# Two steps of an attention branch at a time, keys and values in turn

## The chip, the cores and the metric

One Trainium2 chip, one of its cores. The metric is the device time of one execution in microseconds. Engine names as in the profile: PE (TensorE matmul), PEld (its weight loads), DVE (VectorE), ACT (ScalarE), POOL (GpSimd), SP (the queue that issues most DMAs).

## What is computed

One layer of a decoder trunk over 512 positions, width 1024. A projection feeds two attention branches, A (8 query heads, one key and value head, an indexer that chooses the 128 best keys of each query, a bias by distance) and B (8 heads with up-projected latents, dense causal attention), which are gated, summed, projected and followed by an MLP. Shortened:

```python
h = rmsnorm(x, attn_norm_g)
a_q, a_k, a_v, i_q, i_k, i_w, c_q, c_kv, k_r, g = split_cols(h @ w_in, IN_SIZES)
# A: top_k of the indexer's scores, then attention over the chosen keys
score = einsum('bqh,bqhs->bqs', iw, relu(einsum('bqhd,bsd->bqhs', iq, ik) * 64 ** -0.5))
_, sel = top_k(where(causal, score, -inf), 128)
logits = einsum('bqhd,bqkd->bqhk', q, k[sel]) * 64 ** -0.5 + rel_table[rel_bucket(pos_q - pos[sel])]
y_a = einsum('bqhk,bqkd->bqhd', softmax(where(valid, logits, -1e30)), v[sel])
# B: queries and keys of 64 + 32 (rotary) per head
logits = (einsum('bqhd,bshd->bhqs', q_nope, k_nope) + einsum('bqhr,bsr->bhqs', q_rope, k_rope)) * 96 ** -0.5
y_b = einsum('bhqs,bshd->bqhd', softmax(where(causal, logits, -1e30)), v_b)
gates = sigmoid(g + b_gate)
x = x + (gates[:, :, 0] * (y_a @ w_branch_a) + gates[:, :, 1] * (y_b @ w_branch_b)) @ w_out
x = x + square(relu(rmsnorm(x, mlp_norm_g) @ w_ff1)) @ w_ff2
out = rmsnorm(x, final_norm_g)
```

## The kernel before

The order of PE's instructions is the order in which the program writes them; the other engines' instructions are put in order by the framework, by its own estimate of when each is ready, and each engine then works its list through in that order. Precision is kept by splitting: a matrix is a high part and a rest, and a product is three matmuls (high by high, high by rest, rest by high; `mm3`, L143 to L145, and L239 to L241). A weight is loaded raw by SP (`pre`, L114), ACT writes the high part (L121), DVE the rest (L123); for the weights in `pool_lo` POOL writes the rest. `use` starts this two weights ahead of the matmuls.

The kernel runs in stages. The first projection (L175 to L194) works on slices of `xT` and `wsr` as they land, after `NWARM` small matmuls on zeros. Then come the indexer's scores, the queries of B, and the key and value stage (L553 to L573, about 76 to 91 us): four key chunks (matmuls into `pl`, DVE scales them to `kf`, POOL copies half to `kh`, ACT and DVE write the parts `kth` and `ktl`), then four value chunks that ACT reads into `vb`. PSUM has two buffers `pa`, three `pl`, two `pt` and one `po`.

The B stage (L636 to L652, 91 to 161 us) has 32 steps of one head and one block of 128 queries, and `BL` = 7 more. A step is `b_s0` (three wide matmuls into `pl` and a mask matmul of 16-bit floats, then the softmax: DVE's maximum `nmx`, ACT's exponential `pr`, DVE's reciprocal `rs`, POOL's scaling L592), in each second step of a head `b_q` (four transposes for the next head's queries into `pt`), `b_s1` of the step seven back (transposes of the softmax into `pt`, ACT copies them to `ptb`), and a piece of a gate's projection (`fb`, usually three wide matmuls L239 to L241 into `pa`). After each second head `b_pv` multiplies by the values into `po`, which ACT and DVE read as `ybh` and `ybl`. `topk` gives DVE rounds of the selection (L402, L403), which the framework may put anywhere after their inputs.

The four chunks of A's queries (L670 to L683, 161 to 197 us, the `qa` stage) go into `pa`; DVE scales them to `qf`, ACT and DVE write the parts `qa`; two gate chunks follow. The A stage (L744 to L756, 197 to 275 us) has 32 units of 16 queries, 8 for each block, the longest first. `a_oh` has DVE write four comparisons (`oh`) for a unit; `a_s0` runs two wide matmuls (L705, L706), a mask matmul (L707) and twelve matmuls (L711) of 32 output rows, of which four work side by side, the last two kinds on 16-bit floats, then the softmax; `a_s1` transposes three units later (`LAG`); `fa` is a piece of a gate. After a block `a_av` multiplies by the values. What follows (275 us to the end) is the merging of branches, the output projection and the MLP.

## Time and profile before

| | us |
|---|---|
| median of 3 runs | 723.49 (723.43 to 723.56) |
| profiled execution | 723.43 |
| its span, first to last instruction | 721.7 |
| start to B stage | 91.3 |
| B stage | 69.7 |
| `qa` stage and two gate chunks | 36.0 |
| A stage | 78.4 |
| after it | 446.3 |

A start in a timeline is us from the span's start. A duration of PE includes the time in which a matmul runs beneath the next one, so the cost of one is the distance to the next start. A square bracket holds the idle time of the engine before the instruction and what ended it.

### The profile page before, as it was taken

Reading aid. Unit: us, or ns where it says so; the run is one execution under the profiler, and the core shown is the slowest. Engines: PE = TensorE matmul, PEld = TensorE weight load, DVE = VectorE, ACT = ScalarE, POOL = GpSimd, SP = SyncE. Lnnn points to the kernel's source line nnn. Section 1 sums busy time; section 2 is a strip of 40 time slices with the busy share of each in tenths; the row PEclk is TensorE's granted clock in tenths of the full one; section 3 lists DMA queues with packets and bytes.
Section 4 is the critical chain, followed back from the end, with each engine's and each line's share of the span. In section 5 each row is a group of like instructions: output and inputs, shape, how many; then the busy total and the mean of one; then the engine's idle time right before and its main releaser. Section 6 shows DMA issues by size and latency. Waiting matters only on the chain.

```text
span 721.7 us, 9980 instructions
## 1 busy us (share of the span) xinstructions
PE 707.3 (98%) x3725; PEld 569.7 (79%) x3726; DVE 430.2 (60%) x810; ACT 305.7 (42%) x533; POOL 192.0 (27%) x230
## 2 busy tenths in 40 slices
PE   8999999999899999999999999999999999999996
PEld 7879777778656677888898888888888888888885
DVE  6487899999898865773257353353534425335233
ACT  6466676655544555761156041240514215025013
POOL 2315287530065430332224011020201202012012
PEclk9999999999999999999999999999999999999998
DMA  8532522112221118882046152150412405111002
GB/s 335 202 110 89 153 89 74 45 48 94 84 67 45 46 47 277 322 271 62 1 151 202 56 153 80 66 168 17 167 51 88 145 30 176 29 59 59 0 18 99
DMA packets 25952, 77.16 MB, mean 107 GB/s; under 512 B 3568, under 2 KB 4464, under 8 KB 25904
## 3 DMA queue, kind: packets, MB, share of 16 engines
q1 hardware_dynamic: 24896, 75.19, 31.1%
q10 hardware_dynamic: 1008, 1.34, 0.5%
q8 instruction: 29, 0.48, 0.3%
q14 instruction: 19, 0.16, 0.1%
HBM read 69.31 MB, written 6.29 MB: 105 GB/s over the span
## 4 chain that ended last, share of the span: by engine, by line
PE 87%; DVE 8%; ACT 2%; issue 1%; POOL 1%; DMA 1%; POOLq 0%; SPq 0%; ACTq 0%; DVEq 0%
PE pa L143 10%; PE pa L145 9%; PE pa L144 9%; PE pl L143 9%; PE pl L145 9%; PE pl L144 9%; PE pa L239 4%; PE pa L240 4%; PE pa L241 4%; PE pl L711 2%; DVE sc L403 2%; PE pt L724 2%; PE pa L822 2%; PE pa L821 2%; PE pa L820 2%; DVE m L402 2%
## 5 line engine op out<-in xcount | busy, mean ns | idle before, releaser
L121 ACT ACTIVATE whi<-wraw 128x1024 fp32r<-128x1024 f32 (+1 forms) x103 | 107.9, 1053 | 216.1 <-PE pl L145 88.6
L123 DVE TENSOR_TENSOR wlo<-wraw,whi 128x1024 fp32r<-128x1024 f32 (+1 forms) x98 | 124.9, 1283 | 80.3 <-ACT whi L121 79.8
L875 POOL TENSOR_TENSOR sq<-r 128x512 f32<-128x512 f32 x32 | 49.3, 1543 | 244.3 <-ACT r L873 244.3
L143 PE MATMUL pa<-h2h,whi 128*128 128x512 f32 (+1 forms) x272 | 102.5, 377 | 0.0
L144 PE MATMUL pa<-h2l,whi 128*128 128x512 f32 (+1 forms) x272 | 102.4, 377 | 0.0
L145 PE MATMUL pa<-h2h,wlo 128*128 128x512 f32 (+1 forms) x272 | 102.4, 377 | 0.0
L144 PE MATMUL pl<-wlo,zh 128*128 128x512 f32 (+1 forms) x260 | 100.3, 386 | 0.0
L145 PE MATMUL pl<-whi,zl 128*128 128x512 f32 (+1 forms) x260 | 100.3, 386 | 0.0
L143 PE MATMUL pl<-whi,zh 128*128 128x512 f32 (+1 forms) x260 | 100.3, 386 | 0.0
L890 DVE SCALAR_TENSOR_TENSOR acc<-pl,r,acc 128x512 f32<-128x512 f32 (+1 forms) x65 | 48.2, 741 | 85.8 <-PE pl L145 85.8
L239 PE MATMUL pa<-hh,whi 128*128 128x512 f32 x184 | 79.3, 431 | 2.2 <-DVE qf L673 2.2
L240 PE MATMUL pa<-hl,whi 128*128 128x512 f32 x184 | 72.1, 392 | 0.0
L241 PE MATMUL pa<-hh,wlo 128*128 128x512 f32 x184 | 72.1, 392 | 0.0
L145 PEld LDWEIGHTS pa<-h2h,wlo 128*128 128x128 f32 x272 | 51.2, 188 | 9.4
L143 PEld LDWEIGHTS pa<-h2h,whi 128*128 128x128 f32 x272 | 51.2, 188 | 9.3
L144 PEld LDWEIGHTS pa<-h2l,whi 128*128 128x128 f32 x272 | 51.2, 188 | 9.3
L145 PEld LDWEIGHTS pl<-whi,zl 128*128 128x128 f32 x260 | 48.8, 188 | 9.9
L144 PEld LDWEIGHTS pl<-wlo,zh 128*128 128x128 f32 x260 | 48.8, 188 | 9.8
L143 PEld LDWEIGHTS pl<-whi,zh 128*128 128x128 f32 x260 | 48.8, 188 | 9.8
L592 POOL TENSOR_SCALAR pra<-pra,rs 128x400 f32<-128x400 f32 (+31 forms) x32 | 33.0, 1032 | 61.1 <-DVE rs L591 60.7
L696 DVE TENSOR_SCALAR oh<-posbc,thr 128x400 bf16<-128x400 f32 (+31 forms) x128 | 43.0, 377 | 3.5 <-PE pl L711 3.5
L239 PEld LDWEIGHTS pa<-hh,whi 128*128 128x128 f32 x184 | 35.2, 191 | 11.0 <-issue 6.4
(294 smaller groups left out, 1204.3 us busy)
## 6 DMA issues: line engine op xcount, KB each, us to landing
wraw<-wff SPq DMA_DIRECT2D x64, 512.0 KB, 3.6
wraw<-wF SPq DMA_DIRECT2D x24, 512.0 KB, 3.4
gd<-gt SPq DMA_DIRECT2D x16, 256.0 KB, 2.2
wraw<-wbr SPq DMA_DIRECT2D x8, 512.0 KB, 4.0
wraw<-wout SPq DMA_DIRECT2D x8, 512.0 KB, 5.1
gx<-gd SPq DMA_DIRECT2D x16, 256.0 KB, 3.7
xtok<-x SPq DMA_DIRECT2D x4, 512.0 KB, 9.9
acc<-x SPq DMA_DIRECT2D x1, 2048.0 KB, 9.6
```

The lines of the kernel that those rows point to most:

```text
L121: act.activation(hi, raw, AF.Copy)
L123: eng.tensor_tensor(lo, raw, hi.bitcast(F32), op=ALU.subtract)
L143: pe.matmul(ps, lh, rh, start=(i == 0), stop=False)
L144: pe.matmul(ps, lh, rl, start=False, stop=False)
L145: pe.matmul(ps, ll, rh, start=False, stop=(i == n - 1))
L239: pe.matmul(p, h[:, k], hh[k], start=(k == 0), stop=False)
L240: pe.matmul(p, h[:, k], hl[k], start=False, stop=False)
L241: pe.matmul(p, l[:, k], hh[k], start=False, stop=(k == NK - 1))
L592: pool.tensor_scalar(pr, pr, rs, None, op0=ALU.mult)
L696: dve.tensor_scalar(oh[:, :n], posbc[:, :n], thr[:, 4 * G + q:4 * G + q + 1], None, op0=ALU.is_le)
L875: pool.tensor_tensor(sq, r, r, op=ALU.mult)
L890: dve.scalar_tensor_tensor(acc[:, b, cs], p, r2[:, b:b + 1], acc[:, b, cs], op0=ALU.mult, op1=ALU.add)
```

## The change

Nine edits. (1) The first piece of `xT` is loaded by SP, after the first `wsr`, not by ACT ahead of `vec`; `NWARM` is 52, not 46. (2) `pool_lo` also holds the two gate chunks behind the `qa` stage and the four chunks of A's queries. (3) In the key and value stage a value chunk follows each key chunk; the copy into `kh` is ACT's and the one into the odd heads' `kth` POOL's, in place of the other way round. (4) `b_q` transposes into `po`, not `pt`. (5) The B loop takes two steps at a time: both tiles' wide matmuls, then both masks, then both softmaxes; two `b_s1`; `b_q` with a head's first pair; two fills. `BL` is 6. (6) `topk` gives 26 rounds in the B loop, not 27. (7) The A loop takes two units at a time in the same way (wide, mask, the `L711` kind), with the comparisons of the next pair after it; `LAG` is 2, so `a_s1` runs for the pair before. (8) `oh` has 12 buffers, not 8. (9) `qh` is in the pool of four buffers that `qf` and the gates use.

```diff
--- before.py
+++ after.py
@@ -43,7 +43,8 @@
     return ap.to_broadcast(shape)


-NWARM = 46
+NWARM = 52
+OHB = 12


 def body(nc, tc, ctx, a, out, dbg=lambda name, ap: None):
@@ -129,7 +130,7 @@
     seq += gl[NG1 + 1:NG1 + NG2 + NGB] + [("in", 4 + i) for i in range(4)] + gl[NG1 + NG2 + NGB:]
     seq += [("br", i) for i in range(NK)] + [("ff1", i) for i in range(32)]

-    pool_lo = set(gl[NG1 + NG2:NG1 + NG2 + NGB])
+    pool_lo = set(gl[NG1 + NG2:NG1 + NG2 + NGB + NGQ] + [("in", 4 + i) for i in range(4)])

     def use(key, ahead=2):
         i = seq.index(key)
@@ -151,7 +152,6 @@
     hl = Two(2, F32R, "hl")
     vec = cst.tile([128, 52], F32, name="vec")
     xT = [utile(4 + i, F32, f"xT{i}") for i in range(2)]
-    act.dma_start(xT[0][:, 0:1], a["xT"][:, 0:1])
     act.dma_start(vec, a["vec"])
     warm = cst.tile([128, 1], F32, name="warm")
     dve.memset(warm, 0.0)
@@ -175,8 +175,7 @@
     for nk in (1, 1, 2, 2, 2):
         ks = slice(k, k + nk)
         sp.dma_start(wsr[:, ks], a["wS"][:, ks])
-        if k:
-            sp.dma_start(xT[k // 4][:, k % 4:k % 4 + nk], a["xT"][:, ks])
+        sp.dma_start(xT[k // 4][:, k % 4:k % 4 + nk], a["xT"][:, ks])
         for kk in range(k, k + nk):
             xk = xT[kk // 4][:, kk % 4]
             if kk:
@@ -535,7 +534,7 @@
         sp.dma_start(kth[64:96, h].bitcast(F32), kth[64:96, 0].bitcast(F32))
         sp.dma_start(ktl[h][64:96].bitcast(F32), ktl[0][64:96].bitcast(F32))
     def b_q(h):
-        pt = pt_tile()
+        pt = psO.tile([128, NB, 128], F32, tag="po", name="pq")
         for b in range(NB):
             pe.transpose(pt[:96, b], qtok[:, b, h], ident)
         ptq = pt[:96].rearrange("p a b -> p (a b)")
@@ -557,20 +556,18 @@
         t = t_p.tile([128, S], F32, tag="s2k", name="kf", bufs=4)
         dve.tensor_tensor(t, p, rkbc, op=ALU.mult)
         th = t_p.tile([128, S], F32R, tag="s2k", name="kh", bufs=4)
-        pool.tensor_copy(th[64:128], t[64:128])
+        act.activation(th[64:128], t[64:128], AF.Copy)
         act.activation(kth[0:64, 2 * j], t[0:64], AF.Copy)
-        dve.tensor_tensor(ktl[2 * j][0:64], t[0:64], kth[0:64, 2 * j].bitcast(F32), op=ALU.subtract)
-        act.activation(kth[0:64, 2 * j + 1], th[64:128].bitcast(F32), AF.Copy)
-        kt_last = dve.tensor_tensor(ktl[2 * j + 1][0:64], t[64:128], th[64:128].bitcast(F32), op=ALU.subtract)
-        f2(2)
+        dve.tensor_tensor(ktl[2 * j + 1][0:64], t[64:128], th[64:128].bitcast(F32), op=ALU.subtract)
+        kt_last = dve.tensor_tensor(ktl[2 * j][0:64], t[0:64], kth[0:64, 2 * j].bitcast(F32), op=ALU.subtract)
+        pool.tensor_copy(kth[0:64, 2 * j + 1], th[64:128].bitcast(F32))
+        f2(1.5)
         if j == 2:
             b_q(0)
-    for b in range(NB):
-        sl = slice(b * 128, (b + 1) * 128)
         p = pl_tile()
-        mm3(p, [(zkh[:, sl], zkl[:, sl], ukh[:, 512:1024], ukl[:, 512:1024])])
-        act.activation(vb[:, b], p, AF.Copy, scale=rlat[:, 4 + b:5 + b])
-        f2(1.5)
+        mm3(p, [(zkh[:, cs], zkl[:, cs], ukh[:, 512:1024], ukl[:, 512:1024])])
+        act.activation(vb[:, j], p, AF.Copy, scale=rlat[:, 4 + j:5 + j])
+        f2(2)
     dbg("vb", vb)
     z_st.close()

@@ -596,17 +593,23 @@
     prs, ptbs = {}, {}
     yb = []

-    def b_s0(h, b):
-        n = 128 * (b + 1)
-        pl = pl_tile()
-        qh, ql = (t[:, b * 128:n] for t in qts[h])
-        pe.matmul(pl[:, :n], qh, kth[:, h, :n], start=True, stop=False)
-        pe.matmul(pl[:, :n], qh, ktl[h][:, :n], start=False, stop=False)
-        pe.matmul(pl[:, :n], ql, kth[:, h, :n], start=False, stop=False)
-        pe.matmul(pl[:, b * 128:n], identb, nm0, start=False, stop=True)
-        pr = b2_p.tile([128, n], F32, tag=f"pr{b}", name=f"pr{b}", bufs=3)
-        softmax_rows(pl, n, pr)
-        prs[h, b] = pr
+    def b_s0(h, bb):
+        pls = {}
+        for b in bb:
+            n = 128 * (b + 1)
+            pl = pls[b] = pl_tile()
+            qh, ql = (t[:, b * 128:n] for t in qts[h])
+            pe.matmul(pl[:, :n], qh, kth[:, h, :n], start=True, stop=False)
+            pe.matmul(pl[:, :n], qh, ktl[h][:, :n], start=False, stop=False)
+            pe.matmul(pl[:, :n], ql, kth[:, h, :n], start=False, stop=False)
+        for b in bb:
+            n = 128 * (b + 1)
+            pe.matmul(pls[b][:, b * 128:n], identb, nm0, start=False, stop=True)
+        for b in bb:
+            n = 128 * (b + 1)
+            pr = b2_p.tile([128, n], F32, tag=f"pr{b}", name=f"pr{b}", bufs=3)
+            softmax_rows(pls[b], n, pr)
+            prs[h, b] = pr

     def b_s1(h, j):
         if j == 0:
@@ -631,24 +634,26 @@
         dve.tensor_tensor(ybl[:, h0 // 2], po, ybh[:, h0 // 2].bitcast(F32), op=ALU.subtract)

     f2.flush()
-    BL = 7
+    BL = 6
     fb = Fill(gtake(NGB), 32 + BL)
-    for t in range(32 + BL):
+    for t in range(0, 32 + BL, 2):
         h, i = divmod(t, 4)
         if h < 8:
-            b_s0(h, 3 - i)
-        if i == 1 and h + 1 < 8:
-            b_q(h + 1)
+            b_s0(h, (3 - i, 2 - i))
         h1, j = divmod(t - BL, 4)
         if t >= BL:
             b_s1(h1, j)
-        fb()
+            b_s1(h1, j + 1)
+        if i == 0 and h + 1 < 8:
+            b_q(h + 1)
         if t == 4:
             with tc.issue_after(kt_last.ins):
                 topk(1)
-        elif t > 4 and t % 4:
             topk(1)
-        if j == 1 and h1 >= 2 and h1 % 2 == 0:
+        elif t > 4:
+            topk(1 if i == 0 else 2)
+        fb(2)
+        if j == 0 and h1 >= 2 and h1 % 2 == 0:
             b_pv(h1 - 2)
     fb.flush()
     b_pv(6)
@@ -672,7 +677,7 @@
             t = t_p.tile([128, S], F32, tag="s2k", name="qf", bufs=4)
             dve.scalar_tensor_tensor(t, p, 0.125, r1bc, op0=ALU.mult, op1=ALU.mult)
             tq = t.rearrange("p (g q) -> p g q", q=4)
-            th = a_p.tile([128, S], F32R, tag="qh", name="qh", bufs=1)
+            th = t_p.tile([128, S], F32R, tag="s2k", name="qh", bufs=4)
             act.activation(th[64:128], t[64:128], AF.Copy)
             act.activation(qa[0:64, :, 0, :, j], tq[0:64], AF.Copy)
             act.activation(qa[0:64, :, 1, :, j], tq[64:128], AF.Copy)
@@ -692,29 +697,37 @@
         G = 8 * b + g
         ohs = oht[b, g] = []
         for q in range(4):
-            oh = a_p.tile([128, S], BF16, tag="oh", name="oh", bufs=8)
+            oh = a_p.tile([128, S], BF16, tag="oh", name="oh", bufs=OHB)
             dve.tensor_scalar(oh[:, :n], posbc[:, :n], thr[:, 4 * G + q:4 * G + q + 1], None, op0=ALU.is_le)
             ohs.append(oh)

-    def a_s0(b, g):
-        n = 128 * b + 16 * (g + 1)
-        G = 8 * b + g
-        ohs = oht[b, g]
-        pl = pl_tile()
-        lq = qa[:, 4 * G:4 * G + 4].rearrange("p a b c d -> p (a b c d)")
-        pe.matmul(pl[:, :n], lq, ak[:, 0, :n], start=True, stop=False)
-        pe.matmul(pl[:, :n], lq, ak[:, 1, :n], start=False, stop=False)
-        pe.matmul(pl[:, :n], esel[:, 4 * g:4 * g + 4].rearrange("p a b c d -> p (a b c d)"), nms[b][:, :n],
-                  start=False, stop=False)
-        for i in range(3):
-            for q in range(4):
-                pe.matmul(pl[32 * q:32 * q + 32, :n], dtab[:, i].rearrange("p a b c -> p (a b c)"), ohs[q][:, :n],
-                          start=False, stop=(i == 2))
-        pr = a_p.tile([128, S], F32, tag="pra", name="pra", bufs=5)
-        if g < 7:
-            pool.memset(pr[:, n:128 * (b + 1)], 0.0)
-        softmax_rows(pl, n, pr[:, :n])
-        pas[b, g] = pr
+    def a_s0(us):
+        pls = []
+        for b, g in us:
+            n = 128 * b + 16 * (g + 1)
+            G = 8 * b + g
+            pl = pl_tile()
+            pls.append(pl)
+            lq = qa[:, 4 * G:4 * G + 4].rearrange("p a b c d -> p (a b c d)")
+            pe.matmul(pl[:, :n], lq, ak[:, 0, :n], start=True, stop=False)
+            pe.matmul(pl[:, :n], lq, ak[:, 1, :n], start=False, stop=False)
+        for (b, g), pl in zip(us, pls):
+            n = 128 * b + 16 * (g + 1)
+            pe.matmul(pl[:, :n], esel[:, 4 * g:4 * g + 4].rearrange("p a b c d -> p (a b c d)"), nms[b][:, :n],
+                      start=False, stop=False)
+        for (b, g), pl in zip(us, pls):
+            n = 128 * b + 16 * (g + 1)
+            for i in range(3):
+                for q in range(4):
+                    pe.matmul(pl[32 * q:32 * q + 32, :n], dtab[:, i].rearrange("p a b c -> p (a b c)"),
+                              oht[b, g][q][:, :n], start=False, stop=(i == 2))
+        for (b, g), pl in zip(us, pls):
+            n = 128 * b + 16 * (g + 1)
+            pr = a_p.tile([128, S], F32, tag="pra", name="pra", bufs=5)
+            if g < 7:
+                pool.memset(pr[:, n:128 * (b + 1)], 0.0)
+            softmax_rows(pl, n, pr[:, :n])
+            pas[b, g] = pr

     def a_s1(b, g):
         if g == 0:
@@ -739,20 +752,21 @@
     Fill(gtake(NGQ), 1).flush()
     fa = Fill(gtake(NGA), 34)
     ua = [(b, g) for b in (3, 2, 1, 0) for g in range(8)]
-    LAG = 3
+    LAG = 2
     a_oh(*ua[0])
-    for i in range(len(ua) + LAG):
-        topk(1)
-        if i + 1 < len(ua):
-            a_oh(*ua[i + 1])
+    a_oh(*ua[1])
+    for i in range(0, len(ua) + LAG, 2):
         if i < len(ua):
-            a_s0(*ua[i])
+            a_s0(ua[i:i + 2])
+        for u in ua[i + 2:i + 4]:
+            a_oh(*u)
+        topk(2)
         if i >= LAG:
-            b, g = ua[i - LAG]
-            a_s1(b, g)
-            if g == 0 and b < 3:
-                a_av(b + 1)
-        fa()
+            for b, g in ua[i - LAG:i - LAG + 2]:
+                a_s1(b, g)
+                if g == 1 and b < 3:
+                    a_av(b + 1)
+        fa(2)
     fa.flush()
     fe = Fill(gtake(1), 1)
     fe.flush()
```

## Rows read from the trace of the kernel before

**Rows 1.** Busy time by stretch, B stage and start of A stage: engines, PEclk, DMA.
```profile
91.30:161.00 69.70, 68.12 (x422) 51.75 (x421) 67.96 (x192) 44.27 (x115) 44.59 (x38) 1.00 0.18 65
...
197.00:223.00 26.00, 25.84 (x239) 16.02 (x239) 25.86 (x68) 13.28 (x32) 16.42 (x17) 1.00 0.25 79
```

**Rows 2.** PE's waits, whole span: us in total, times, longest.
```profile
PE pa L239 <- DVE qf L673: 2.2, 2, 1.2
PE pl L143 <- ACT vb L572: 1.4, 1, 1.4
...
PE pt L616 <- ACT ptb L618: 0.8, 2, 0.5
PE pl L605 <- DVE qtl L549: 0.8, 1, 0.8
```

**Rows 3.** Timeline of PE, one step of the A stage: start, us, instruction.
```profile
213.45 0.83 PE L711 MATMUL pl<-oh,dtab 128*32 128x512 bf16 x12 [0.16 <-DVE oh L696]
214.22 0.66 PE L724 MATMUL pt<-ident,pra 128*128 128x128 f32 x4
214.63 0.48 PE L239 MATMUL pa<-hh,whi 128*128 128x512 f32 x1
214.95 0.39 PE L240 MATMUL pa<-hl,whi 128*128 128x512 f32 x1
215.18 0.39 PE L241 MATMUL pa<-hh,wlo 128*128 128x512 f32 x1
...
215.53 0.29 PE L706 MATMUL pl<-ak,qa 128*128 128x272 f32 x1
215.66 0.29 PE L707 MATMUL pl<-nm,esel 128*128 128x272 bf16 x1
215.88 0.53 PE L711 MATMUL pl<-oh,dtab 128*32 128x272 bf16 x12
```

**Rows 4.** Timeline of PE, two runs of transposes in the B stage.
```profile
107.98 0.28 PE L616 MATMUL pt<-ident,pr 128*128 128x128 f32 x1
108.01 0.48 PE L239 MATMUL pa<-hh,whi 128*128 128x512 f32 x1
...
109.15 0.61 PE L616 MATMUL pt<-ident,pr 128*128 128x128 f32 x4
109.52 0.48 PE L239 MATMUL pa<-hh,whi 128*128 128x512 f32 x1
```

**Rows 5.** Timeline of all engines, softmax of one unit of the A stage.
```profile
200.41 0.86 PE L711 MATMUL pl<-oh,dtab 128*32 128x432 bf16 x12
...
203.32 0.62 ACT L589 ACTIVATE pra<-pl,nmx 128x432 f32<-128x432 f32 x1 [1.58 <-DVE nmx L587]
...
204.83 1.57 POOL L592 TENSOR_SCALAR pra<-pra,rs 128x432 f32<-128x432 f32 x1 [0.44 <-DVE rs L591]
```

**Rows 6.** Timeline of all engines, one `b_pv` and its reading by DVE.
```profile
135.41 2.38 PE L628 MATMUL po<-ptb,vb 128*64 128x512 f32 x16
...
139.18 0.68 DVE L631 TENSOR_TENSOR ybl<-po,ybh 128x512 fp32r<-128x512 f32 x1
```

**Rows 7.** Timeline of all engines, key and value stage.
```profile
81.58 0.69 DVE L564 TENSOR_TENSOR ktl<-kf,kh 64x512 fp32r<-64x512 f32 x1
...
82.21 2.40 POOL L123 TENSOR_TENSOR wlo<-wraw,whi 128x1024 fp32r<-128x1024 f32 x1 [2.63 <-ACT whi L121]
...
84.10 1.04 DVE L562 TENSOR_TENSOR ktl<-kf,kth 64x512 fp32r<-64x512 f32 x1
...
85.66 0.63 ACT L563 ACTIVATE kth<-kh 64x512 fp32r<-64x512 f32 x1 [2.00 <-POOL kh L560]
```

**Rows 8.** Groups of DVE by line, 161 to 197 us.
```profile
L123 DVE TENSOR_TENSOR wlo<-wraw,whi 128x1024 fp32r<-128x1024 f32 x6 | 7.2, 1208 | 0.0
```

**Rows 9.** Timeline of DVE and PE, third slice of the first projection.
```profile
10.25 1.41 DVE L187 SCALAR_TENSOR_TENSOR hl<-xT,vec,hh 128x512 fp32r<-128x512 f32 x2 [0.47 <-ACT hh L186]
...
11.34 0.39 PE L193 MATMUL pl<-hl,wsh 128*128 128x512 f32 x1
```


## Prediction

> **What bounds the kernel now.** I read the stage table first, then PE's waits, then one period of each attention stage on PE. In the B stage (91 to 161 us) and the first part of the A stage (197 to 223 us) PE is occupied for 68.1 of 69.7 and 25.8 of 26.0 us, and DVE for 68.0 and 25.9 [rows 1]: both are nearly full, PE's clock is 1.00 throughout. All waits of PE that the profile names make a few microseconds, of which four concern the change: 2.2 us for `qf` (L673), 1.4 for `vb` (L572), 0.8 for `ptb` (L618), 0.8 for `qtl` (L549) [rows 2]. So PE's order sets the time, and what can be won is (a) these waits and (b) PE's own time per step. For (b) the reader should look at starts, not at durations, since matmuls overlap: a start-to-start distance is what one costs.
>
> In the A period [rows 3] `L240` follows its like and takes 0.23 us (214.95 to 215.18); `L239`, of the same size but the first after transposes, takes 0.32 (214.63 to 214.95): 0.09 for the change of kind. `L706` takes 0.13 (215.53 to 215.66) for 272 columns and the mask `L707`, as long, 0.22 (215.66 to 215.88), because the 32-column kind follows it: 0.09. The twelve `L711` of 512 columns are three rounds of four side by side; three rounds at 0.22 are 0.66, and the transposes start after 0.77 (213.45 to 214.22): 0.11. A run of transposes is the exception: a run of one takes 0.03 (107.98 to 108.01), a run of four 0.37 (109.15 to 109.52) [rows 4], so each further one costs 0.11, and joining two runs loses about 0.08 in B. In A, where a run of four takes 0.41 [rows 3], I put that loss at 0.03.
>
> The Trainium skill says otherwise (TensorE: Matmul & The Clock Gate, "Step-by-step: what each phase is for"): weight loads are pulled ahead of running matmuls, so that the next weights load beneath them. By that alone, longer runs would save nothing. Within a kind the trace agrees (0.23 per matmul), at a change of kind it does not (0.32).
>
> **The change part by part.** Gains are counted positive.
>
> *A in pairs* (`a_s0` over two units, then two `a_s1`, then two fills). Per pair one entry into the wide matmuls (0.09), one mask to `L711` change (0.09), one `L711` to transpose change (0.11) fall away, less 0.03: 0.26 x 16 pairs = 4.2 us [rows 3]. Against it stands a shorter lead. `LAG` falls from 3 steps to one pair. A unit's softmax takes long there: the 432-column unit's `L711` run 200.41 to 201.27, its scaling on POOL ends at 206.40 (204.83 + 1.57): 5.1 us [rows 5]. In the pair order PE has between the second unit's end and its transposes: eight transposes (0.85), two fills (1.3, from 0.23 per matmul), the next pair's `a_s0` (about 2.6 from rows 3 scaled to 432 columns): 4.75. Short by 0.35 in each of the four widest pairs: 1.4; I take 1.0, since DVE begins with twelve comparisons in hand (`OHB`) instead of eight. In the later blocks the softmax is shorter with the columns, and nothing is charged, but the last pair has only the fills before its transposes: 0.4. A: 4.2 - 1.4 = +2.8 (bounds -1 to 4.2: the low end is 0.35 in all 16 pairs, 5.6).
>
> *B in pairs.* One entry (0.09) and about 0.03 around the mask fall away, 0.08 is lost in the joined transposes: 0.04 x 18 = 0.7 at most; I take +0.5 [rows 3, 4]. `b_q` moves from the two `pt` buffers to the single `po` buffer. That frees the transposes of `b_s1`: the 0.8 us of `ptb` goes [rows 2]. It also moves ahead in the head, by about a step, so I let 0.5 of the 0.8 of `qtl` go [rows 2]; DVE's list there is still full of top-k rounds. The price: `b_q` now needs `po`, which the `b_pv` just before it (t = 14 and 22) fills. A `b_pv` issues from 135.41, ends at 137.79, and DVE has read it at 139.86 [rows 6]: 2.1 us. Before `b_q` PE has only a pair of `b_s0` (1.3 us: six matmuls of 512 and 384 columns, two masks) and three transposes (0.25): 0.5 short, twice: -1.0 (bounds 0 and -2.4). Behind the waiting transpose stand two fills and the next pair, that is all of PE. Then the three `pl` buffers: a pair holds two, so the second tile of the next pair needs the first tile of this one read by ACT, with transposes (0.5), fills (1.4) and one tile (0.5) between, 2.4 us in place of some 4.7. `pr` takes 0.62 on ACT [rows 5] and `nmx` on DVE about as much, 1.2 when nobody is ahead of them, but DVE is full [rows 1]. I charge 0.04 per pair, 0.7 in all (bounds 0 and 0.3 x 19 = 5.7). The other step, `BL` 7 to 6, takes one step off a list whose matmuls are the same: 0. B: 0.5 + 0.8 + 0.5 - 1.0 - 0.7 = +0.1 (bounds -5 to 2).
>
> *Keys and values in turn.* PE waited 1.4 us for ACT to read a `pl` tile into `vb` [rows 2]; ACT itself had waited 2.00 us for POOL's copy `kh` (85.66), which stood on POOL behind a 2.40 us weight piece (82.21 to 84.61) [rows 7]. The change gives this copy to ACT and leaves POOL one that nothing on PE needs before head 1, and values take turns with keys, so ACT and DVE empty alternate tiles. With the matmul's own slower start it is 1.5 us (bounds 0 and 1.6). If POOL were late again, only `kth` of odd heads would be late. `kt_last` moves behind more DVE work, hence the first top-k round; rounds have until the A stage: 0. The `b_q(0)` inside it has `po` free: 0.
>
> *Six weight pieces from DVE to POOL, `qh` in the four-buffer pool.* In the `qa` stage DVE does six of these pieces, 7.2 us [rows 8], and the 2.2 us of `qf` are DVE being late [rows 2]. At least four of the six go. By the count the whole 2.2 goes. But POOL and DVE hold each other up: `ktl` L564 takes 0.69 alone, the same size at L562 takes 1.04 when it starts within POOL's piece, and ends 0.53 after that has ended (84.61) [rows 7]. The `qa` subtractions read two SBUF tiles as `ktl` does. Each j may lose up to a piece's 2.4 us there, against 1.2 saved. I take +1.6 (bounds 0 and 2.2). SP's loads of later weights wait for the slower piece, but there are two chunks of matmuls (10.9 us) ahead: 0.
>
> The Trainium skill's SBUF — State Buffer ("SBUF: two separate sides") calls this an exclusive lock, for the whole instruction, between GpSimd and a DVE operation with two SBUF inputs. It speaks against this part; by it alone the term could be 0 and the sum 1.6 us smaller. The trace agrees in the one place above.
>
> *The start.* `xT`'s first piece goes behind `wsr` on SP's queue, `vec` is first on ACT's. `hh` needs both; if it then precedes the second `wsh` on ACT, PE starts earlier. It cannot gain much: `hl` of the third slice is done about 10.95 (two in 1.41 from 10.25), PE wants it at 11.34 [rows 9]: at most 0.4. If ACT keeps its order, the second `wsr` is one issue later: -0.4. I take +0.2. Six more warm-up matmuls end before data can be there: 0.
>
> Sum: 2.8 + 0.1 + 1.5 + 1.6 + 0.2 = 6.2 us. The profiled execution took 723.43 (span 721.7, 1.7 around it); the median of the runs is 723.49. So 717.2 in either count, since everything after the A stage is matmuls back to back that shift as a whole.
>
> **The rivals.**
> 1. *Buffers take it all (slower).* Place: the three `pl` buffers in both attention stages. Each pair waits for `nmx` and `pr` of the last pair's first tile. For it: DVE full in both stages [rows 1], lead cut by half. Against: DVE is rid of up to six weight pieces, and the order of its list may place `nmx` first. Over 35 pairs, 0.7 us of it is charged already; from 0.24 us a pair ((6.2 + 0.7 + 1.5) / 35) the kernel is measurably slower; at 0.4 it costs 14 and gives 717.2 + 14 - 0.7 = 730.5.
> 2. *Longer runs save nothing* (the loads are exposed per unit, not per run): A and B lose 4.7: 721.9. For it: I infer the saving from single changes. Against: within runs the loads are hidden in every row.
> 3. *Nothing new is late:* without the charges (A 1.4, `po` 1.0, `pl` 0.7, POOL 0.6) 3.7 more: 713.5. For it: eased DVE. Against: rows 5 and 6.
> 4. *The clock falls.* In this trace transposes stand among matmuls and the granted clock is 1.00 [rows 1]. If longer runs of them let it fall to 1.2 GHz through the 26 us of the first A stretch, that stretch would take up to twice as long: 743 (an estimate). The Trainium skill (TensorE: Matmul & The Clock Gate, "Part 4: PE-mode transpose") says transposes don't count as busy; no row here shows it.
>
> **How the numbers follow.** Forecast 0.60, rival 3 0.16, rival 2 0.10, rival 1 0.12, rival 4 0.02. The forecast's own bounds, taken half way each, are 713.5 to 721; with most of rivals 3 and 2 the range is 712.5 to 722.5, and what is left out is rival 1, rival 4 and the ends of the others. A measurement here can tell about 0.2%, 1.45 us: faster is below 722.0. The forecast, rival 3 and half of rival 2 lie there: 0.81. Within: 0.08, slower: 0.11.
>
> **What would show it.** Right: `L239` entries at 0.32 half as many; the period of two A units shorter by 0.26; no wait for `vb`, `ptb`; `qf` waits small or gone; new waits of `b_q` for `ybl` about 0.5 us, of the widest A transposes for POOL. Wrong: PE waiting at the second tile of a pair for `pr` (rival 1), entries as many or as dear as before (rival 2), a granted clock under 1.00 in A (rival 4), or the gain lying past the A stage.

## The result, and the profile after

The changed kernel takes 728.58 us against 723.46 for the kernel before (medians of four runs each, side by side): ratio 1.0072 [1.0054, 1.0089], slower by 5.1 us where 6.2 us of gain were forecast. The profiled execution has a span of 726.8 us, 5.0 more than before.

Where it went is read from the stage windows. Cut at the first PE instruction of each stage (keys and values; B; `qa`; A), first the kernel before, then the changed one. A row is the stretch, its length, busy time (instructions) of PE, weight loads, DVE, ACT and POOL, the granted clock, and DMA.

```profile
75.00:91.28 16.28, 14.88 (x69) 12.00 (x68) 14.47 (x23) 10.24 (x16) 5.14 (x5) 1.00 0.62 170
91.28:160.78 69.50, 67.92 (x421) 51.54 (x420) 67.76 (x192) 44.21 (x114) 44.54 (x37) 1.00 0.18 65
160.78:196.26 35.48, 33.31 (x146) 26.98 (x145) 32.59 (x64) 18.89 (x21) 0.58 (x5) 1.00 0.24 82
196.26:275.31 79.05, 78.82 (x720) 51.34 (x719) 62.64 (x200) 38.57 (x105) 36.42 (x55) 1.00 0.19 61
```

```profile
75.32:89.88 14.56, 14.56 (x70) 12.08 (x69) 12.73 (x17) 8.27 (x13) 5.56 (x4) 1.00 0.71 190
89.88:163.75 73.87, 69.50 (x422) 54.35 (x420) 71.77 (x201) 44.83 (x117) 51.00 (x40) 0.98 0.18 62
163.75:198.04 34.29, 33.06 (x147) 27.06 (x146) 30.68 (x58) 18.88 (x20) 9.82 (x10) 1.00 0.28 93
198.04:280.37 82.33, 77.34 (x721) 52.19 (x720) 64.26 (x195) 35.86 (x105) 37.87 (x55) 0.98 0.17 56
```

Keys and values lose 1.72 us and `qa` 1.19, as meant; B grows by 4.37 and A by 3.28; the start is 0.32 later; everything past A is 446.4 us in both. In A, PE's busy time did fall (78.82 to 77.34), but PE now stands still for 5 us that it did not before. What it stands still for (the view of PE's waits, after; it answers to [rows 2]):

```profile
PE pt L737 <- POOL pra L589: 4.8, 7, 1.8
PE pl L602 <- ACT pr L586: 2.9, 3, 2.4
PE pq L539 <- DVE ybl L634: 1.5, 2, 0.8
PE pa L238 <- DVE qf L678: 1.2, 1, 1.2
```

The waits for `vb`, `ptb` and `qtl` of [rows 2] are gone and `qf` is down from 2.2 to 1.2. Three new ones, 9.2 us together, took their place. All three happen where the prediction looked for them: `pra` and `pl` at a far higher price (4.8 against 1.4, 2.9 against 0.7), `ybl` nearer to its own (1.5 against 1.0).

**The start of B.** The timeline of PE, DVE and ACT around the second pair, after (start, duration, engine, line; in brackets the idle time and what ended it):

```profile
93.28 0.28 PE L604 MATMUL pl<-kth,q 96*128 96x256 f32 x1
95.91 0.47 PE L602 MATMUL pl<-kth,q 96*128 96x128 f32 x1 [2.35 <-ACT pr L586]
...
90.86 1.00 DVE L562 TENSOR_TENSOR ktl<-kf,kth 64x512 fp32r<-64x512 f32 x1
91.79 0.68 DVE L401 MAX8 m<-sc 128x8 f32<-128x512 f32 x1
93.77 0.68 DVE L401 MAX8 m<-sc 128x8 f32<-128x512 f32 x1
94.38 1.14 DVE L584 TENSOR_REDUCE nmx<-pl 128x1 f32<-128x512 f32 x2
...
92.21 1.05 ACT L122 ACTIVATE whi<-wraw 128x1024 fp32r<-128x1024 f32 x1
93.75 1.28 ACT L586 ACT_TABLE_LOAD   x1
95.08 0.69 ACT L586 ACTIVATE pr<-pl,nmx 128x512 f32<-128x512 f32 x1
```

The fourth score tile needs the first of three `pl` buffers. PE is there at 93.56 us. But DVE had the last key's remainder until 91.86, then a top-k round, a gate's product and the start of the next round, so `nmx` starts at 94.38; and ACT had weight pieces, a query's copy and the table for the exponential until 95.03. In the kernel before PE wanted that tile at 95.72, 2.2 us later, and did not wait:

```profile
95.72 0.22 PE L603 MATMUL pl<-kth,q 96*128 96x128 f32 x1
```

**The clock.** That stop has a price of its own (windows just before, in and after):

```profile
92.40:95.90 3.50, 1.16 (x7) 0.83 (x5) 3.46 (x8) 3.44 (x6) 3.50 (x2) 1.00 0.36 98
95.90:99.30 3.40, 3.39 (x11) 2.90 (x12) 3.37 (x11) 1.11 (x5) 2.31 (x3) 0.51 0.75 264
99.30:102.70 3.40, 3.40 (x20) 2.83 (x20) 3.40 (x9) 1.60 (x6) 2.66 (x3) 0.99 0.08 28
```

PE was busy 1.16 of 3.50 us; then the granted clock is 0.51 (1.2 GHz) for 3.4 us, in which PE gets through 11 instructions where the next 3.4 us see 20. The same follows the stop at 222 us in A.

What this adds to a stop shows where the stop is the same and the clock is not. late_rounds, one of the kernels below, has the A loop of the changed kernel and the same waits for `pra`, but its clock stays at 1.00 there, and A takes 80.86 us in place of 82.33 (its wait, then its A window):

```profile
PE pt L739 <- POOL pra L591: 4.8, 7, 1.8
196.53:277.39 80.86, 76.01 (x722) 50.97 (x720) 64.29 (x195) 35.75 (x105) 37.84 (x55) 1.00 0.17 57
```

So 1.5 of the 3.3 us that A lost are the clock's. In B, after_light and lag4_light below share the loop and a stop of 2.33 us; B takes 73.71 where the clock is then at half for 6.8 us, and 72.37 where it is for 3.4: 1.3 us for 3.4. Of the 7.7 us lost in A and B, some 2.8 would be the clock's (an estimate from these two pairs of runs).

**The A stage.** All engines around the last wide pair, after:

```profile
213.46 1.46 PE L722 MATMUL pl<-oh,dtab 128*32 128x496 bf16 x24
213.94 2.49 DVE L701 TENSOR_SCALAR oh<-posbc,thr 128x272 bf16<-128x272 f32 x5
216.35 0.66 DVE L584 TENSOR_REDUCE nmx<-pl 128x1 f32<-128x496 f32 x1
218.16 1.82 POOL L589 TENSOR_SCALAR pra<-pra,rs 128x496 f32<-128x496 f32 x1 [2.16 <-DVE rs L588]
219.93 0.92 POOL L728 MEMSET pra<- 128x112 f32 x3
220.84 1.56 POOL L589 TENSOR_SCALAR pra<-pra,rs 128x512 f32<-128x512 f32 x1
222.45 1.12 PE L737 MATMUL pt<-ident,pra 128*128 128x128 f32 x4 [1.76 <-POOL pra L589]
```

The pair's scores are complete at 214.92 (213.46 + 1.46), and the second unit leaves POOL at 222.40: 7.5 us. The prediction had 5.1 [rows 5] against 4.75 of PE's work. The extra is a queue at two engines: DVE does five comparisons before it looks at the scores (`nmx` at 216.35), and since both units of a pair are ready together, POOL's second scaling stands behind the first and three `memset`s.

### The profile page after: what moved, and what is told of

Its sections match the earlier page's. It is cut to its first block, busy times and chain, and to the rows that moved or that the text cites. A ratio compares the mean times of both kernels' runs of the same rounds, so it can differ in the third digit from the quotient of the medians.

```text
span 726.8 us, 9995 instructions
## 1 busy us (share of the span) xinstructions
PE 707.5 (97%) x3731; PEld 573.4 (79%) x3732; DVE 434.0 (60%) x804; ACT 301.1 (41%) x533; POOL 208.4 (29%) x236
## 4 chain that ended last, share of the span: by engine, by line
PE 76%; DVE 15%; issue 3%; POOL 2%; ACT 1%; DMA 1%; SPq 0%; POOLq 0%; ACTq 0%; DVEq 0%
PE pa L144 9%; PE pa L145 9%; PE pa L146 9%; PE pl L145 9%; PE pl L146 9%; PE pl L144 9%; DVE sc L402 3%; DVE m L401 3%; PE pa L238 3%; PE pa L239 3%; PE pa L240 2%; DVE nmx L584 2%; DVE oh L701 2%; PE pa L835 2%; PE pa L836 2%
## 5 line engine op out<-in xcount | busy, mean ns | idle before, releaser
L124 DVE TENSOR_TENSOR wlo<-wraw,whi 128x1024 fp32r<-128x1024 f32 (+1 forms) x92 | 118.6, 1299 | 81.6 <-ACT whi L122 81.4
L238 PE MATMUL pa<-hh,whi 128*128 128x512 f32 x184 | 77.2, 420 | 1.2 <-DVE qf L678 1.2
L701 DVE TENSOR_SCALAR oh<-posbc,thr 128x400 bf16<-128x400 f32 (+31 forms) x128 | 46.2, 408 | 5.8 <-PE pl L722 5.8
L589 POOL TENSOR_SCALAR pra<-pra,rs 128x400 f32<-128x400 f32 (+31 forms) x32 | 34.7, 1092 | 40.1 <-DVE rs L588 40.0
```

Of the source, the lines that this page charges most:

```text
L124: eng.tensor_tensor(lo, raw, hi.bitcast(F32), op=ALU.subtract)
L238: pe.matmul(p, h[:, k], hh[k], start=(k == 0), stop=False)
L589: pool.tensor_scalar(pr, pr, rs, None, op0=ALU.mult)
L701: dve.tensor_scalar(oh[:, :n], posbc[:, :n], thr[:, 4 * G + q:4 * G + q + 1], None, op0=ALU.is_le)
```

## The experiments

All changes are against the kernel named; a stage time is the span between the same marks as above. KV stands for the stage of keys and values. Times are medians; [ ] is the interval of the ratio to the kernel before, run side by side. Stage times are of one profiled execution, which took within 0.7 us of the median, except in late_rounds (725.49), keys_ahead_lag4 (726.69) and b_single (728.73).

| kernel | us | ratio | KV | B | `qa` | A |
|---|---|---|---|---|---|---|
| before | 723.46 | 1 | 16.28 | 69.50 | 35.48 | 79.05 |
| changed | 728.58 | 1.0072 | 14.56 | 73.87 | 34.29 | 82.33 |
| lag4 | 724.95 | 1.0022 [1.0013, 1.0032] | 14.56 | 73.86 | 34.29 | 79.11 |
| unit_order | 724.77 | 1.0021 [1.0012, 1.0031] | 14.56 | 73.84 | 34.30 | 78.61 |
| late_rounds | 724.72 | 1.0019 [1.0010, 1.0029] | 14.56 | 73.09 | 33.54 | 80.86 |
| b_single | 726.31 | 1.0035 [1.0020, 1.0049] | 14.56 | 74.78 | 34.10 | 80.79 |
| before_light | 720.02 | 0.9953 [0.9937, 0.9970] | 16.27 | 69.09 | 32.78 | 78.82 |
| after_light | 720.03 | 0.9954 [0.9939, 0.9969] | 14.56 | 73.71 | 32.78 | 76.55 |
| lag4_light | 717.90 | 0.9924 [0.9909, 0.9939] | 14.56 | 72.37 | 32.78 | 74.67 |
| unit_light | 721.83 | 0.9980 [0.9970, 0.9989] | 14.56 | 72.38 | 32.78 | 78.61 |
| kv_only | 722.96 | 1.0000 [0.9987, 1.0012] | 14.56 | 71.58 | 34.71 | 79.05 |
| kv_before_lag4 | 723.57 | 1.0001 [0.9992, 1.0011] | 16.30 | 71.77 | 32.78 | 79.13 |
| keys_ahead_lag4 | 725.59 | 1.0033 [1.0020, 1.0046] | 14.56 | 75.61 | 33.87 | 79.03 |
| pieces_back_lag4 | 725.59 | 1.0030 [1.0018, 1.0042] | 14.56 | 73.62 | 33.41 | 80.62 |
| bq_pt | 724.65 | 1.0008 [0.9998, 1.0018] | 16.30 | 73.15 | 32.78 | 78.97 |
| after_sign | 723.10 | 0.9991 [0.9981, 1.0000] | 14.56 | 73.83 | 32.78 | 78.70 |
| single_sign | 721.52 | 0.9969 [0.9957, 0.9981] | 16.27 | 69.52 | 33.59 | 78.79 |
| units_sign | 723.13 | 0.9995 [0.9985, 1.0004] | 16.26 | 69.53 | 35.50 | 78.56 |
| pairs_sign | 719.69 | 0.9941 [0.9927, 0.9956] | 16.27 | 69.52 | 35.46 | 75.25 |
| pairs_sign_lo | 716.86 | 0.9906 [0.9890, 0.9923] | 16.28 | 69.52 | 32.80 | 75.24 |

**A: the lead, and the order.** lag4 gives the changed kernel a lead of two pairs (the transposed rows get a smaller tile to make room, not shown here); unit_order keeps that lead and its buffers but goes through the units one by one.

```diff
-    LAG = 2
+    LAG = 4
-... name="pra", bufs=5)
+... name="pra", bufs=7)
```

> The changed kernel with the transposes of the A stage two pairs behind instead of one (LAG 4; seven buffers for the softmax rows, and the transposed rows of blocks 0 and 2 in a smaller tile to make room). Theory (the lead is too short: DVE and POOL finish a softmax after PE wants it, PE idles 4.8 us for pra and its clock then falls): the waits for pra go, the clock stays at 1.00 around 222 us, the A stage (first A matmul to the branch stage) takes 75 us in place of 82.3, the whole about 721.5. Rival (the longer runs or a full DVE cost the time, and the waits only show where): A stays at 79 us or more, the waits move to another tile, the whole 725 to 728.5.

> The kernel of LAG 4 with PE's A stage unit by unit, as before the change: wide, mask and narrow matmuls, transposes and a fill of one unit, then of the next; the lead is the same four units. Only the length of the runs of one kind differs. Theory (a change of kind costs PE 0.26 us a pair): the A stage is 4.2 us longer than with LAG 4 in pairs, about 79 us, the whole 4 us longer than that kernel. Rival (longer runs save nothing): the same within 1 us.

The longer lead gives A back 3.2 us (82.33 to 79.11), 1.5 of them the clock's, so the short lead was one cause. But pairs (79.11) are then no better than units (78.61): with a whole lead the saved switches are nowhere to be seen. What PE waits for in lag4's A is now the softmax and the comparisons:

```profile
PE pl L712 <- ACT pra L586: 1.2, 2, 1.0
PE pl L722 <- DVE oh L701: 1.1, 3, 0.4
```

The next four kernels leave work out to see why: half of the top-k rounds, and one comparison stands for all four queries of a unit.

```diff
-        for q in range(4):
+        for q in range(1):
...
-            ohs.append(oh)
+            ohs.extend([oh] * 4)
```

> The kernel before with a light DVE: half of the top-k rounds are left out, and one comparison of a unit of A serves all four narrow matmuls, so the choice of keys and the bias are not the reference's. In the runs so far DVE worked 68.2 of the 69.5 us of B before the change and 71.9 of 73.9 after it. Theory (DVE's list is the bound of B and of the wide blocks of A, so what PE saves is not seen): PE is now the bound; the B stage takes 67 us, the A stage (first A matmul to the branch stage) 78.3, its own waits gone; the whole about 718. Rival (DVE only looks full since rounds fill its gaps): both stages within 0.7 us of before (69.5 and 79.05).

> The changed kernel with the same light DVE as the one above (half of the rounds, one comparison for four). Theory (DVE bound): the changes of kind now show; A 75.5 us in place of 82.3, B 67 in place of 73.9, the whole 714, that is faster than the light kernel before by 4. Rival (the lead and the three pl and one po buffers are too short whatever DVE does): waits for pra and pl stay at over 2 us each, A at 79 or more, B at 71 or more, the whole 720 or more.

> The kernel with LAG 4 and the light DVE. Theory: nothing waits in A, the pairs give all of 4.2 us, A 74.5 us. Rival (longer runs save nothing): A at 78 us or more.

> PE's A stage unit by unit with LAG 4 and the light DVE; only the runs are shorter than in the kernel above. Theory (0.26 us a pair for changes of kind, hidden so far beneath DVE): 4.2 us longer in A than the kernel above, about 78.5 us. Rival (changes of kind cost nothing when merged): within 1 us of it.

With DVE light, pairs take 74.67 and units 78.61: 3.9 us for the longer runs, against 4.2 in the sum. Units take 78.61 whether DVE is light or not, so units are held by PE, and pairs with a full DVE are held by DVE. before_light went its rival's way: neither A (78.82) nor B (69.09) moved by 0.7 us. In after_light the wait for `pra` is down to 0.6 us, but B keeps its stop of 2.3 us at the start (73.71; 72.37 in lag4_light): half of the rounds gone, and B's loss is still there. The same without leaving anything out: one of the four comparisons goes to ACT, as the sign of the difference (1 or -1); the other three count 2 and the table is halved (and the threshold is moved by a half, so that the sign is never 0), which shifts a row of scores by a constant and leaves its softmax as it is.

```diff
-            dve.tensor_scalar(oh[:, :n], posbc[:, :n], thr[...], None, op0=ALU.is_le)
+            if q == 3:
+                act.activation(oh[:, :n], posbc[:, :n], AF.Sign, scale=-1.0, bias=th)
+            else:
+                dve.tensor_scalar(oh[:, :n], posbc[:, :n], th, 2.0, op0=ALU.is_le, op1=ALU.mult)
```

single_sign is the kernel before with this alone; pairs_sign adds A in pairs with the long lead; units_sign has the same lead and buffers unit by unit.

> The kernel before with only the one comparison moved to ACT, order and lead of before. Before's A is held by PE and DVE alike (PE 25.9 of 26 us), so with PE's work unchanged A stays at 78 to 79, qa may lose 0.5 to 1.5; time 721.5 to 723.5. If DVE alone held A in the kernel before, A falls to 75 or 76 without any pairs, and the switches cost nothing.

> The same as pairs_sign with only the order of A changed to unit by unit, the lead (four units) and the tiles kept. Theory: A 78 to 79, 3 to 4 us more than pairs_sign. Rival: equal to pairs_sign within 0.5 us.

> The kernel before with A in pairs, a lead of two pairs (LAG 4) and one of the four comparisons of each unit on ACT (as a sign of the difference, with the table halved and the other three worth 2, which shifts each row of scores by a constant); start, KV and B stage as before. Theory (the switches are saved, but DVE hides it): A 74.7 to 76.5 instead of 79.05, everything else as before, time 719 to 721.5. Rival (longer runs save nothing where the work is whole): A 78 to 79, time 722.5 to 724.

The A windows of lag4, units_sign and pairs_sign, in this order:

```profile
197.75:276.86 79.11, 76.69 (x722) 51.31 (x720) 64.64 (x195) 35.67 (x105) 37.88 (x53) 1.00 0.17 58
```

```profile
196.88:275.44 78.56, 78.56 (x721) 51.12 (x719) 55.59 (x167) 48.62 (x134) 34.87 (x53) 1.00 0.20 62
```

```profile
196.25:271.50 75.25, 75.24 (x721) 50.86 (x719) 57.12 (x167) 46.32 (x134) 36.88 (x53) 1.00 0.19 64
```

The reader is to compare the second and third figure: in lag4 PE is busy 76.69 of 79.11, in the other two all the time. (So 2.4 of the 3.9 us between lag4 and pairs_sign are idle time; the other 1.4 lie in what the view counts as busy.) The order alone makes 78.56 into 75.25: 3.3 us for longer runs, with the computation whole. And single_sign (78.79) shows that relieving DVE gave the old order next to nothing in A (79.05 to 78.79); its gain lies in `qa` (33.59), and why units_sign, at 35.50, lacks it is not told apart. Neither change moves A by itself; both together do.

after_sign eases DVE in the changed kernel and leaves its short lead.

> The changed kernel with one comparison of four on ACT, nothing else. Theory (A lost by a short lead together with a full DVE): A 76 to 78 instead of 82.3, waits for POOL's pra 0.5 to 2 us instead of 4.8; KV and B as after the change (14.6, 73 to 74); qa 33 to 34; time 721.5 to 724. Rival (the lead alone): A stays at 80 or more and the time over 725.

A falls from 82.33 to 78.70, with 3.1 us of waits for POOL left. The theory's place was right, its sizes were not (A 76 to 78, waits of 0.5 to 2 us). The clock stays at 1.00 in this A and in lag4's, so both are to be set against the 80.8 us that the changed loop takes at a full clock (80.86 in late_rounds, 80.79 in b_single). From there the lead alone (lag4) is worth 1.7 us, DVE alone 2.1, and both 5.6 (75.25 of pairs_sign, whose other stages are those of before): more than the sum, so they are not two separate losses.

**B: pairs or turns.** b_single puts the B loop of before into the changed kernel; late_rounds holds the first top-k round behind the second `nmx`.

> The changed kernel with the B loop of before: one step at a time, BL 7, queries transposed into pt. Theory (the pairs of B lose by pl and po what the A stage does not lose): the B stage takes 69.5 us in place of 73.9, no fall of the clock in B, the whole 724.2. Rival (the keys and values in turn end later on DVE, and that alone starves the first steps): a wait of 2 us at the start of B stays, the whole 727 or more.

> The changed kernel with DVE's first top-k round queued behind the second maximum of the first pair of B, not behind the last key's rest. Theory (DVE's list has a round and a half, a gate's copy and the last key ahead of the first maximum, so the third tile's buffer is late): PE's 2.4 us wait at 93 us falls under 0.7 us and the clock stays at 1.00 there, the B stage takes 70.3 in place of 73.9 us, the whole 725. Rival (three pl buffers are too few for pairs whatever DVE does, or the load of the exponential's table, 1.28 us, holds it): a wait of 1.5 us or more stays, the whole 727.5 to 728.6.

b_single needs care. Its ten executions range from 723.89 us, at a mean granted clock of 0.998, to 728.73, at 0.993, and the profiled one is the last of these. In it PE stops for 0.9 and 1.1 us at the start of B and the clock is at half for 6.8 us afterwards, which at 1.3 us for 3.4 makes some 2.7 of the 74.78 (an estimate). The three executions at 0.998 took 723.89 to 724.87, about what the theory said. So the old loop does take back a part of B's loss; but the 72.1 that remain by the estimate are more than the 69.50 of before, so the loop over B is not the only cause. late_rounds was a miss worth reading. Its DVE, ACT and PE at the same place:

```profile
92.41 1.14 DVE L586 TENSOR_REDUCE nmx<-pl 128x1 f32<-128x512 f32 x2
...
93.77 1.28 ACT L588 ACT_TABLE_LOAD   x1
95.07 0.69 ACT L588 ACTIVATE pr<-pl,nmx 128x512 f32<-128x512 f32 x1
...
95.90 0.33 PE L604 MATMUL pl<-kth,q 96*128 96x128 f32 x1 [2.31 <-ACT pr L588]
```

`nmx` is 2.0 us earlier and PE's stop is as long: ACT's own list ends at 95.05 all the same. Two engines were late there for reasons of their own. That its median, 724.72, meets the theory's 725 is luck: against the changed kernel's profile A gave 1.5 us (the clock), B and `qa` 0.8 each. The loop over keys and values was then exchanged alone, in both directions.

kv_only is the kernel before with the new loop; kv_before_lag4 is lag4 with the old loop, so that B runs in pairs behind it.

> The kernel before with only the loop over keys and values replaced by that of the change. Theory (turns make the keys late): the KV stage shrinks by 1.7 us as after the change, 16.3 to 14.6, but the last key is now followed by one value chunk instead of four, so DVE is still splitting keys when B starts; PE stops 1 to 2.5 us at one of the first tiles of B and B takes 72 to 74 us instead of 69.5; time 724 to 726. Rival (the pairs make the stop, the turns are a clean gain): B 69.5 to 70, time 721.8 to 722.3.

> The changed kernel with the loop over keys and values of before, and with the longer lead in A (LAG 4). Theory (turns make the keys late): KV 16.3, no stop of PE at the start of B, granted clock 1.00 in B, B 68.5 to 70 in pairs; A 79.1 as with the longer lead; span 720 to 721.5. Rival (the pairs themselves cost B its 4 us): B stays at 72.5 to 74, span 724 to 726.

Each theory was half right. Turns alone cost B 2.1 us (69.50 to 71.58), which is more than the 1.7 they save in KV. Pairs, with three more weight pieces on POOL in that stretch, cost B 2.3 (69.50 to 71.77); the pieces alone cost nothing there (pairs_sign_lo below has them with the old loop, and B takes 69.52). In neither kernel's profile does the clock fall. That 2.1 and 2.3 make the changed kernel's 4.4 is luck: its B also holds the 3.4 us at half clock, some 1.3 us, so the waits of the two overlap in part. keys_ahead_lag4 runs the keys one step ahead (key, key, value, key, value, key, value, value).

> The changed kernel with the longer lead in A, and the order key, key, value, key, value, key, value, value. Theory: two value chunks behind the last key cover DVE's work on it, so both are had: KV 14.6 to 15.0, B 69 to 71, span 718.5 to 721. Rival (the pairs cost B): B 72.5 to 74 and span about 723, as with the turns.

It failed: B takes 75.61, with a stop of 2.7 us and 6.8 us at half clock behind it, twice the changed kernel's. The last key's remainder is done at 90.92 us there, 0.9 earlier than in the changed kernel. So the late keys are not what PE waits for: DVE fills the time with top-k rounds and takes `nmx` at 94.95, and `pr` starts at 95.66. That is the pattern of all of them. The first `pr` starts at 94.07 us in the kernel before and at 94.22 in kv_only, though PE is there 1.7 us sooner; in pairs it starts at 95.41 with the old loop and at 95.08 with the new one. The KV stage only brings PE sooner to engines that are not sooner ready.

The waits of PE in kv_before_lag4 that are B's, and the same of bq_pt, which puts `b_q` back into the two `pt` buffers:

```profile
PE pl L604 <- ACT pr L588: 1.5, 2, 1.0
PE pq L539 <- DVE ybl L636: 1.3, 2, 0.9
```

```profile
PE pt L539 <- ACT ptb L623: 1.8, 5, 0.4
PE pl L604 <- ACT pr L588: 1.0, 1, 1.0
PE pt L621 <- DVE qtl L548: 0.8, 1, 0.8
```

> kv_before_lag4 (B in pairs, keys and values as before, lead of two pairs) with the query transposes back in the two pt buffers. If the move to po costs more than it frees: the waits for ybl (1.7 us over two places) go and at most 1.2 for ptb and 0.9 for qtl come back: B 70.5 to 71.8 against 71.77. If the pairs' loss lay in po: B at 69.5 to 70. The waits of score tiles for pr (2.9 us in six places) stay in either case.

The move to `po` was a gain: without it B takes 73.15, 1.4 us more, not less. The five waits for `ptb` before the query transposes are what pairs would have cost there. The view names only waits of some length; by distances between PE's starts in kv_before_lag4 the second tile of a pair is late in six places (1.2, 0.3, 0.2, 0.7, 0.3 and 0.3 us, 2.9 in all).

**The six weight pieces.** pieces_back_lag4 is lag4 with the pieces on DVE again; pairs_sign_lo is pairs_sign with them on POOL.

> The changed kernel with the longer lead in A, and with the six weight pieces back on DVE. If DVE gained nothing by giving them away because POOL's pieces and DVE hold each other up: comparisons, key remainders and masks get shorter beside the pieces, qa stage 34.3 to 35.5, A 79.1 or less, span 722.5 to 724.5 against 723.2. If the pieces were a relief for DVE: qa stage 36 or more, A 80 or more, span 725 to 728.

> pairs_sign with the six weight pieces on POOL as in the change. If they relieve DVE where it is late: qa stage 32.8 to 33.5 instead of about 35.5, A as in pairs_sign, time 1.5 to 2.5 us under it. If what DVE is freed of comes back as slower work beside POOL: the sum of qa and A within 0.7 us of pairs_sign.

In lag4 the move is worth 0.6 us over `qa` and A together (114.03 to 113.40). `qa` is even shorter with the pieces back (33.41), and A longer (80.62): work that DVE does not do in one stage it does in the next. With DVE eased it is worth 2.7 (35.46 to 32.80), more than its upper bound. What cost it in the changed kernel is one place (DVE, then POOL):

```profile
184.16 2.12 DVE L405 TENSOR_SCALAR nm<-sc 128x256 bf16<-128x256 f32 x1
186.20 0.68 DVE L678 SCALAR_TENSOR_TENSOR qf<-pa,r1bc 128x512 f32<-128x512 f32 x1
...
183.74 2.39 POOL L124 TENSOR_TENSOR wlo<-wraw,whi 128x1024 fp32r<-128x1024 f32 x1 [5.43 <-ACT whi L122]
```

The mask `nm` took 0.29 us in the kernel before:

```profile
L406 DVE TENSOR_SCALAR nm<-sc 128x256 bf16<-128x256 f32 x1 | 0.3, 294 | 0.0
```

Here it starts inside POOL's piece, ends 0.15 us after it, and `qf` behind it is late: that is the 1.2 us of `qf` left in the waits. The Trainium skill (SBUF — State Buffer, "SBUF: two separate sides") counts `tensor_scalar` among the DVE operations that can take the ports shared with GpSimd, and lets whichever of the two starts second wait for the whole of the first; these rows agree.

pairs_sign_lo, at 716.86 us, is the fastest: the A pairs and the POOL pieces of the change, with the lead and a DVE that leave room for them, and the KV and B stages of before.

## Why the prediction was wrong, point by point

- *A, +2.8 forecast, -3.3 measured.* The 4.2 for the switches was right in kind and nearly in size (3.3 to 3.9). The charge of 1.4 was the failed step: 7.1 was lost (82.33 against 75.25), 5.6 in waits and 1.5 by the clock after a wait, for which the sum had no term. The charge put one unit's softmax [rows 5] against PE's work between, as if each unit had POOL and DVE for itself. Both units of a pair finish at once, so the second waits for the first on POOL, and DVE's comparisons for the next pair go ahead of `nmx`. The low bound missed it too (with 5.6 as the most it should be -1.4, not -1), because the forecast read DVE's 25.9 of 26 us [rows 1] as a remark, not as a second bound: PE could be 4 us faster in A only if DVE was.
- *B, +0.1 forecast, -4.4 measured*, inside the stated bounds (-5 to 2; the terms' own low ends add up to -6.3). Pairs, by kv_before_lag4: the freed `ptb` and `qtl` were worth 2.1 by the starts on PE (1.3 in the sum); `po` cost 1.7 (1.0); the net of that move is 1.4 by bq_pt. The `pl` buffers cost 2.9 instead of 0.7: right place, wrong size. The step that set 2.4 us of PE's work against 1.2 for `nmx` and `pr` "when nobody is ahead of them" held in most pairs and not where a table load, weight pieces and rounds stood ahead. What longer runs gave is what remains of the 2.27 us: -2.9 - 1.7 + 2.1 leaves 0.2 to 0.3 gained (0.5 in the sum). The other 2.1 of the changed kernel come with the turns: the stop at the fourth tile grows from 1.04 to 2.35 us, and the clock is at half behind it (some 1.3).
- *Keys and values, +1.5 forecast, +1.7 in the stage and -0.4 over KV and B.* The wait for `vb` went as described. That nothing else would be late ("rounds have until the A stage: 0") was the failed step. PE came 1.7 us earlier to a stage whose first softmax DVE and ACT could not start earlier.
- *Six pieces, +1.6 forecast, +1.2 measured.* The right size in the stage, and both mechanisms were there: the relief (2.7 with DVE eased) and the hold-up by POOL (1.2 left at `qf`).
- *The start, +0.2 forecast, -0.3 measured*, is not told apart: this stretch varies from 75.0 to 75.8 us among the kernels, with either start, 76.4 once.
- *Rivals.* Rival 1 was the nearest: slower, buffers in both attention stages. Its place (`pl`) was right for B; in A it was `pra`, behind POOL. Rival 2 is refuted by units_sign and pairs_sign. Rival 4's clock did fall, twice for 3.4 us, not because of transposes (in pairs_sign, with the same runs of eight, it stays at 1.00) but after PE's stops: a wait's price was counted at its length alone, and some 2.8 of the 7.7 us lost in A and B are the clock's.

## What to carry to other kernels

Where two engines are both busy nearly all of a stage, a saving on one is worth only the slack of the other: price the second engine's list before the first one's gain. Doing two steps at a time halves the number of switches, but makes two results fall due at once; ask which single queue then serves both, and lengthen the lead with the group. A stop of PE can cost more than its length: the clock behind it added 1.3 to 1.5 us here, in some executions and not in others. A wait removed just ahead of a stage border is worth nothing until the engines behind the border can start earlier too.

## What the runs showed that was not expected

- The clock: after stops of 1.8 and 2.4 us on PE the granted clock was 0.5 for 3.4 us in the changed kernel, and after one of 2.3 in lag4; matmuls of 512 columns then start 0.43 us apart (97.81 to 98.24 in the changed kernel) instead of 0.23. The length of a stop does not settle it: at the start of B kv_only and b_single both show stops of 0.9 and 1.1 us three microseconds apart, and only b_single's clock fell, for 6.8 us; and the stop of 1.76 us in A is followed by 3.4 us at half in the changed kernel and by none in late_rounds and b_single. What decides it is not shown.
- The order of PE's work changed the length of DVE's: 96 comparisons took a mean of 398 ns in units_sign and 427 in pairs_sign, 128 of them 377 before and 408 after. The longer ones lie beside POOL's scalings: of the changed kernel's of 512 columns, one that began inside such a scaling (213.16 us, POOL at work from 212.55 to 216.00) took 0.79 us, where the mean of the four is 0.55; not each one is held up (another, begun at 212.76 inside the same scaling, took 0.48), but of the 58 of 128 that began while POOL stood idle none was. In the changed kernel DVE was rid of six pieces (7.2 us, [rows 8]) and was busy with comparisons for 3.2 us more (43.0 to 46.2).
